# A decoder layer in float32 on one core: an order of issue worked out by the kernel itself, and 130 k pairs by seven products in place of 36

## The chip, the core and the metric

The program runs on one NeuronCore of one Trainium2 chip. A core has a matrix engine (TensorE, PE in the profile), a vector engine (VectorE, DVE), an activation engine (ScalarE, ACT), a general engine (GpSimd, POOL) and an engine that issues transfers (SyncE, SP). Each engine takes its own list of instructions strictly in the order of the program; semaphores hold an instruction back until its inputs are there and its output buffer is free. SBUF is the on-chip memory with 128 partitions, PSUM holds the sums of TensorE in eight banks of 128 x 512 float32 values. The metric is the device time of one execution in microseconds (us), the median over several.

## The reference, cut to what is computed

One layer on 256 tokens with `D = 2048`. All is float32.

```python
h = rmsnorm(x, g_mix)
x_r, g_r, q, k, v, gate_r, gate_a = split(h @ w_in)      # 2816, 2816, then five of 2048
xc = causal_depthwise_conv(x_r, conv_w, conv_b)
y_r = (gelu(g_r) * rg_lru(xc, ...)) @ w_rnn_out          # gates by block-diagonal weights, then a scan over time
q, k = head_rmsnorm(q, q_gain), head_rmsnorm(k, k_gain)  # 16 heads of 128
y_a = stick_breaking_attention(q, k, v) @ w_attn_out
x = x + (sigmoid(gate_r) * y_r + sigmoid(gate_a) * y_a) @ w_o
g, u = split(rmsnorm(x, g_ffn) @ w_ffn_gu)               # 2 x 5632
x = x + (silu(g) * u) @ w_ffn_down
x = x + sigmoid(rmsnorm(x, g_ple) @ w_ple_gate) * (p @ w_ple_proj)
```

Some 350 MB of weights are read once, for 256 tokens.

## The kernel before

**A product of two float32 numbers in three.** TensorE reads float32 operands in a rounded form (`F32R`). Every operand is therefore split into a high part (`AF.Copy` on ScalarE into an `F32R` tile) and a low part (the difference, on VectorE), and a product is the sum of three: high by high, high by low, low by high. For the weights this happens on the chip: `Stream` walks over `CHUNKS` (eight weight tiles of 128 x 128, 512 KB), `dma_to` issues the loads on SP into `p32` (4 buffers), `split_to` issues the two splits into `phl` (4 buffers for each half; lines 230 and 231), `need` keeps the loads 4 and the splits 3 chunks ahead of the use. Weights are packed on the host in the order of `PLAN`.

**Two ways to multiply.** In the recurrent part (x_r and g_r, 22 column tiles each) the weights are stationary: `dense` multiplies a weight tile by 512 columns (the high and low part of 256 tokens, line 425) and its low part by 256 (line 429). The gates (`rnn_gates`) use `mm3` (lines 407 to 409, 256 columns). Everything else has the tokens stationary: `prod` (lines 495 to 497) loads 128 tokens of one k tile as the stationary operand and streams 512 columns of weights, three matmuls for one product. A `group` is 1024 columns of the output: four PSUM banks `q2, q4, q3, q8` (two halves of columns by two halves of tokens), and for each of its k tiles four products.

**Seven products in place of eight.** Two neighbouring k tiles and the two halves of columns make a 2 x 2 block of weights; with the two halves of tokens that is eight products. Strassen's scheme in Winograd's form makes it seven, with sums of weights. `half_sums` forms the sums of tokens; the sums of weights come from transfers that add (`add`, line 214: a load on GpSimd's queue with `accum_op` into the tile that has just been split). In a group that has it, two k pairs are done so (`QP`, by default pairs 2 and 3): slots `"11", "22", "T1", "21", "T2", "T3", "T4"` among the plain slots of `SEVEN`, `SEVEN_FIRST` and `LONG`, each slot one chunk of 1024 columns and two products. Four more PSUM banks (`late`) hold the products that several outputs need, and five VectorE additions and a copy join them at `"T3"`. 18 groups have it: both of `ro`, `v` and `wo`, all 11 of `gu` and the first of `pg`. q, k, the two gates, `ao` and `dn` are plain.

**Order.** The code issues in the order of its loops: the recurrent pairs with four gate blocks among them, `ro`, `v`, q and k blocks with the attention's four steps hooked in by `ATT_AT`, the gate, `ao`, `wo`, the FFN (`gu` and `dn` in four quarters), `pg`. The framework (`schedule_with_timeline_sim=True`) then shifts instructions by its own model. Tiles come from pools by kind (`NT`: A, B, C, X, T), each with its number of buffers. Nine matmuls on zeros (line 537) stand ahead of the first product.

## Time and profile before

| | |
|---|---|
| median of 3 runs | 1896.65 us (1896.46 to 1898.97) |
| the profiled execution's own time | 1897.7 us |
| its span in the trace | 1895.9 us |
| mean granted TensorE clock | 0.999 |
| instructions in the trace | 24167 |
| HBM read, written | 386.00 MB, 2.10 MB |

The page gives each engine's busy time, a strip of 40 slices, the DMA queues, the chain of work that ended last, and the costliest groups of instructions. A group's row names line, engine, operation, `out<-in` by the program's tiles, the shape and the count, then busy time and the mean duration of one, then the engine's idle time just before these instructions and what ended it. Durations overlap: a matmul of 512 columns is shown with 390 ns, while the next one starts 227 ns after it; what an engine can do is read from the distance of starts. TensorE's weight loads (PEld) run beside its matmuls. A few records of matmuls can be missing.

### The profile page before, as it was taken

To read this page: it belongs to the slowest core of one execution; us is meant where nothing else is said; L and a number is where in the kernel's file an instruction comes from. 1 tells how busy PE (TensorE), PEld (TensorE's weight loads), DVE (VectorE), ACT (ScalarE), POOL (GpSimd) and SP (SyncE) were. 2 spreads that over 40 slices of the span, in tenths; PEclk is the share of its full clock that TensorE was granted. 3 is DMA by queue.
4 is the path that set the end of the run, shared out by engine and by line. 5 is a ranking of instruction groups with operands and counts; after the bars stand their busy time and mean duration, and the time that the engine had idled before them with its cause. 6 is when DMAs were issued, how large, how long until landed. Compare 5 with 4: busy or idle time off the path is not lost.

```text
span 1895.9 us, 24167 instructions
## 1 busy us (share of the span) xinstructions
PE 1883.8 (99%) x9045; PEld 1583.6 (84%) x9045; DVE 1274.3 (67%) x1546; ACT 1112.1 (59%) x1447; POOL 63.6 (3%) x81
## 2 busy tenths in 40 slices
PE   8999999999999999999999999999999999999998
PEld 7988888888888888888888888888888888888887
DVE  7867686866766576665567776665666566665674
ACT  7878686874455576676345665543554355544663
POOL 0000000000010000000000000000000000000000
PEclk9999999999999999999999999999999999999999
DMA  7565556677777554555677878776887688766674
GB/s 246 179 199 189 196 176 192 208 234 211 243 202 211 190 166 157 166 156 178 198 269 208 251 227 239 223 222 190 233 236 220 190 232 232 204 196 191 212 201 152
DMA packets 109557, 389.69 MB, mean 206 GB/s; under 512 B 12288, under 2 KB 12672, under 8 KB 109440
## 3 DMA queue, kind: packets, MB, share of 16 engines
q1 hardware_dynamic: 98928, 350.38, 55.4%
q0 software_dynamic: 10368, 37.75, 11.8%
q8 instruction: 71, 1.16, 0.2%
q14 instruction: 46, 0.38, 0.1%
q10 hardware_dynamic: 144, 0.01, 0.0%
HBM read 386.00 MB, written 2.10 MB: 205 GB/s over the span
## 4 chain that ended last, share of the span: by engine, by line
PE 97%; DVE 1%; ACT 1%; DMA 1%; issue 0%; SPq 0%; DVEq 0%; ACTq 0%
PE ps L496 26%; PE ps L495 26%; PE ps L497 26%; PE ps L425 8%; PE ps L429 4%; PE ps L408 1%; PE ps L409 1%; PE ps L407 1%; PE ps L994 1%; DMA w<-in_w_dram 0%; PE ps L934 0%; PE ps L785 0%; DVE T L300 0%; ACT L306 0%; ACT T L306 0%
## 5 line engine op out<-in xcount | busy, mean ns | idle before, releaser
L231 DVE TENSOR_TENSOR wlo<-w,whi 128x1024 fp32r<-128x1024 f32 (+3 forms) x606 | 731.3, 1215 | 426.3 <-ACT whi L230 424.8
L230 ACT ACTIVATE whi<-w 128x1024 fp32r<-128x1024 f32 (+3 forms) x606 | 635.3, 1053 | 560.1 <-PE ps L497 494.5
L496 PE MATMUL ps<-wlo,B 128*128 128x512 f32 x1130 | 440.7, 390 | 0.2 <-DVE wlo L231 0.2
L497 PE MATMUL ps<-whi,B 128*128 128x512 f32 x1130 | 440.4, 390 | 0.0
L495 PE MATMUL ps<-whi,B 128*128 128x512 f32 x1130 | 390.8, 392 | 0.0
L496 PE MATMUL ps<-wlo,A 128*128 128x512 f32 x946 | 368.9, 390 | 0.0
L497 PE MATMUL ps<-whi,A 128*128 128x512 f32 x946 | 368.2, 390 | 0.0
L495 PE MATMUL ps<-whi,A 128*128 128x512 f32 x946 | 352.7, 391 | 0.0
L497 PEld LDWEIGHTS ps<-whi,B 128*128 128x128 f32 x1130 | 212.2, 188 | 44.0
L496 PEld LDWEIGHTS ps<-wlo,B 128*128 128x128 f32 x1130 | 212.3, 188 | 43.6 <-DVE wlo L231 0.7
L495 PEld LDWEIGHTS ps<-whi,B 128*128 128x128 f32 x1130 | 212.2, 188 | 43.7
L497 PEld LDWEIGHTS ps<-whi,A 128*128 128x128 f32 x946 | 177.6, 188 | 36.9
L495 PEld LDWEIGHTS ps<-whi,A 128*128 128x128 f32 x946 | 177.7, 188 | 36.3
L496 PEld LDWEIGHTS ps<-wlo,A 128*128 128x128 f32 x946 | 177.7, 188 | 35.9 <-DVE wlo L231 0.4
L231 DVE TENSOR_TENSOR wlo<-X,whi 128x1024 fp32r<-128x1024 f32 x126 | 154.3, 1224 | 66.8 <-ACT whi L230 62.0
L230 ACT ACTIVATE whi<-X 128x1024 fp32r<-128x1024 f32 x126 | 133.7, 1061 | 93.1 <-PE ps L497 55.7
L425 PE MATMUL ps<-A,whi 128*128 128x512 f32 x704 | 171.0, 392 | 1.7 <-ACT whi L230 1.7
L425 PEld LDWEIGHTS ps<-A,whi 128*128 128x128 f32 x704 | 129.2, 189 | 26.9 <-ACT whi L230 2.1
L214 POOL DMA_DIRECT2D X<-in_w_dram x72 | 61.4, 853 | 1752.2 <-DVE wlo L231 1577.7
L300 DVE TENSOR_TENSOR T<-ps,T 128x512 f32<-128x512 f32 (+1 forms) x160 | 91.1, 610 | 27.6 <-ACT T L306 16.1
L429 PEld LDWEIGHTS ps<-A,wlo 128*128 128x128 f32 x704 | 90.5, 191 | 7.1 <-DVE wlo L231 3.5
L429 PE MATMUL ps<-A,wlo 128*128 128x256 f32 x704 | 92.2, 283 | 2.9 <-DVE wlo L231 2.9
(158 smaller groups left out, 1419.8 us busy)
## 6 DMA issues: line engine op xcount, KB each, us to landing
w<-in_w_dram SPq DMA_DIRECT2D x584, 512.0 KB, 4.1
X<-in_w_dram POOLq DMA_DIRECT2D x72, 512.0 KB, 5.5
X<-in_w_dram SPq DMA_DIRECT2D x54, 512.0 KB, 5.1
w<-in_w_dram SPq DMA_DIRECT2D x16, 448.0 KB, 3.2
C<-in_x_dram SPq DMA_DIRECT2D x8, 256.0 KB, 3.8
out_dram<-T SPq DMA_DIRECT2D x8, 256.0 KB, 2.9
C<-in_xT_dram SPq DMA_DIRECT2D x7, 256.0 KB, 7.9
w<-in_w_dram SPq DMA_DIRECT2D x4, 320.0 KB, 3.5
```

The lines of the kernel that those rows point to most:

```text
L214: self.nc.gpsimd.dma_start(self.raw[o], self.src[a], accum_op=ALU.add)
L230: self.hi_ins = self.nc.scalar.activation(hi[:, :c], t[:, :c], AF.Copy)
L231: self.lo_ins = self.nc.vector.tensor_tensor(lo[:, :c], t[:, :c], hi[:, :c].bitcast(F32), ALU.subtract)
L300: nc.vector.tensor_tensor(o, a, b, op)
L407: nc.tensor.matmul(o, wt[0], xh, start=start, stop=False)
L408: nc.tensor.matmul(o, wt[0], xl, start=False, stop=False)
L409: nc.tensor.matmul(o, wt[1], xh, start=False, stop=stop)
L425: nc.tensor.matmul(pss[e], wt[0], rhs(xs, k), start=(k == 0), stop=(k == n - 1))
L429: nc.tensor.matmul(pss[e][:, :256], wt[1], rhs(xs, k)[:, :256], start=False, stop=False)
L495: nc.tensor.matmul(ps, x[0], wh, start=start, stop=False)
L496: nc.tensor.matmul(ps, x[0], wl, start=False, stop=False)
L497: nc.tensor.matmul(ps, x[1], wh, start=False, stop=stop)
```

## The change

The kernel is written anew around the same arithmetic (1103 lines become 1389). What it does:

**An own order.** `build` records every operation as an `Op` in a `Program`: engine, an assumed duration, the tiles that it reads and writes. `deadlines` gives each a due time from TensorE's order, `schedule` plays the five engines and one transfer server against these durations and hands out buffers, and `emit` issues the operations sorted by the start found there. The framework's own shifting is off (`manual_schedule`). The assumed durations are constants of the file (`PE_NS`, `LOAD_US`, `ADD_US` and the formulas in `vec` and `act`).

**All stages with tokens stationary.** x_r and g_r become groups too: five groups of 512 + 512 columns and a short one of 256 + 256. Their results have tokens on partitions, so x_r is turned by TensorE before the convolution (`conv`) and g_r before the last product (`finish`), 22 turns of four transposes each. The scale of the first norm is read from x in token layout: eight more loads of 256 KB (`xq`), squared with a row sum. `dense`, `evac`, `scaled`, the norm's matmuls (lines 478 and 565) and the nine matmuls on zeros go.

**130 k pairs by seven products**, in 65 blocks of two pairs (18 before): `CFG` lists them. Now also x_r with g_r (one block in the first group, two in the next four), `ro` (2 blocks in each group), gate_r and `v` (2), q and k (1), gate_a (1), `wo` (1), `gu` (2), `dn` (2, 2 and 1 in its three parts), `pg` (2); only `ao` and the short group have none.

**Half of the sums on VectorE.** Per block of two pairs there were four adding transfers; now there are two (T1 and T3) and two additions of 128 x 1024 on VectorE (T2 and T4, in place).

**One chained bank.** The products for several outputs go into one bank `U`, one after another, and ScalarE or VectorE takes the running sum out between them (`ja`, `je`, `jc`, `jd`): five banks for a group in place of eight.

**One pool.** All tiles of 1024 columns share 42 slots (`L`), all of 512 columns 22 (`H`); the scratch for GpSimd's descriptors is cut to 1024 bytes for each partition (`SCRATCH`). FFN: three parts of 16, 16 and 12 k tiles in place of four.

In the built programs TensorE has 9039 matmuls before and 8478 after (of 512 columns 7437 and 7498, of 256 columns 1238 and 532, of 128 columns 344 and 432), VectorE 1546 and 1887 operations, ScalarE 1299 and 1551 activations with 68 and 57 loads of a function table, GpSimd 72 and 130 adding transfers, SP 687 and 648 transfers. The weight splits go from 732 to 873 of each kind.

```diff
+LOAD_US, ADD_US, DMA_LEAD, DMA_TAIL = 1.575 / 512, 2.96 / 512, 1.3, 1.2
+PE_NS = {512: 0.2268, 256: 0.1200, 128: 0.1090}
...
+    def vec(self, n, emit, reads, writes, pointer=False, single=False, name="", **kw):
+        d = 0.062 + 0.001048 * n * (0.5 if single else 1) + (0.06 if pointer else 0)
+        return self.op("DVE", d, 0.125, emit, reads, writes, name=name, **kw)
...
+def schedule(prog, room, window, lag=0.0):
...
+                if e == "PE":
+                    for _, _, o in ready[e]:
+                        if rank[o.n] - head > window:
+                            break
+                        if can(o):
+                            pick = o
+                            break
...
+    return sorted(prog.ops, key=lambda o: (o.start, o.n))
...
-    def add(self, mode):
-
-        m, o, a = {"11": ("T1", "11", "T1"), "T1": ("T2", "11", "22"), "T2": ("T4", "11", "21"),
-                   "22": ("T3", "22", "T1")}.get(mode, (None,) * 3)
-        if m:
-            self.nc.gpsimd.dma_start(self.raw[o], self.src[a], accum_op=ALU.add)
-            self.raw[m] = self.raw[o]
...
+    def group(w, cols, ks, pairs, sums, tokens, how, hooks=None, lead=0):
...
+        q2, q4, q3, q8 = (psum("q") for _ in range(4))
+        U = psum("u") if nd else None
...
+            if m in ("T1", "T3"):
+                if how(m) == "dma":
+                    pr.add(raw.all, chain["b12", dp], 512, name="add")
...
+            if m in ("T2", "T4"):
+                other = chain["22" if m == "T2" else "21", dp]
+                tt(raw.all, raw.all, other.all, ALU.add, name="sum")
+            w_ = weights(raw, 1024, "s")
...
+                    if m == "11":
+                        a = tile("ja", "H")
+                        act(a.all, U.all, AF.Copy, name="ja")
+                    elif m == "T1":
+                        e = tile("je", "H")
+                        tt(e.all, a.all, U.all, ALU.subtract, name="je")
...
-    warm = psum()
-    for i in range(9):
-        nc.tensor.matmul(warm, ones_r, w1t[0], start=True, stop=True)
...
-        for c in range(nc_):
...
-            for f in ((low, wide) if c % 2 or c == nc_ - 1 else (wide, low)):
...
+    for b in range(NBK):
+        xr_group(b, 4, later_hooks(b))
...
-QP = {"ro": (7, 8)}
+CFG = dict(lead=8, x=[4, 5, 6, 7], xr=[[6, 7]] + [[4, 5, 6, 7]] * 4, ro=[0, 1, 2, 3], gtr=[4, 5, 6, 7], v=[4, 5, 6, 7], qk=[4, 5], gta=[4, 5],
+           ao=[], wo=[0, 1], gu=[0, 1, 2, 3], dn=[[0, 1, 2, 3], [8, 9, 10, 11], [16, 17]], pg=[0, 1, 2, 3],
+           how=lambda m: "dma", att0=4, every=9, at=(0, 4, 10, 16), turn=[4, 5, 6, 7])
+SCRATCH = 1024
+ROOM = {"L": 42, "H": 22, "P": 8}
+WINDOW = 60
...
-    with _tile.TileContext(nc, schedule_with_timeline_sim=True) as tc:
-        tile_hybrid_block(tc, *args)
+    with _tile.TileContext(nc) as tc:
+        with tc.manual_schedule():
+            trace(nc, tc, pr, order, args)
```

## The prediction, made blind

> **What bounds the kernel now.** First the page: the engines' busy time, then the chain that ended last.

> ```profile
> span 1895.9 us, 24167 instructions
> PE 1883.8 (99%) x9045; PEld 1583.6 (84%) x9045; DVE 1274.3 (67%) x1546; ACT 1112.1 (59%) x1447; POOL 63.6 (3%) x81
> PE 97%; DVE 1%; ACT 1%; DMA 1%; issue 0%; SPq 0%; DVEq 0%; ACTq 0%
> PE ps L496 26%; PE ps L495 26%; PE ps L497 26%; PE ps L425 8%; PE ps L429 4%; PE ps L408 1%; PE ps L409 1%; PE ps L407 1%; PE ps L994 1%; DMA w<-in_w_dram 0%; PE ps L934 0%; PE ps L785 0%; DVE T L300 0%; ACT L306 0%; ACT T L306 0%
> ```

> TensorE is the bound, and 97% of the chain is its matmuls. A busy TensorE can still be one that runs slowly, so next the groups by shape, for counts, and the chain and the timeline, for the distance of starts.

> ```profile
> L496 PE MATMUL ps<-wlo,B 128*128 128x512 f32 x1130 | 440.7, 390 | 0.2 <-DVE wlo L231 0.2
> L496 PE MATMUL ps<-wlo,A 128*128 128x512 f32 x946 | 368.9, 390 | 0.0
> L425 PE MATMUL ps<-A,whi 128*128 128x512 f32 x704 | 171.0, 392 | 1.7 <-ACT whi L230 1.7
> L429 PE MATMUL ps<-A,wlo 128*128 128x256 f32 x704 | 92.2, 283 | 2.9 <-DVE wlo L231 2.9
> L496 PE MATMUL ps<-wlo,X 128*128 128x512 f32 x160 | 62.4, 390 | 0.8 <-DVE wlo L231 0.8
> ```

> ```profile
> 38.52 3.65 PE ps L425 x16
> 42.17 1.91 PE ps L429 x16
> ...
> 653.97 1.03 PE L785 MATMUL ps<-ident,T 128*128 128x128 f32 x8
> ...
> 1433.24 1.07 PE L495 MATMUL ps<-whi,B 128*128 128x512 f32 x4
> ```

> A 512-column matmul starts (1.07 - 0.39) / 3 = 0.227 us after the one before, a product of three takes 0.68 us. Sixteen stationary weight tiles take 3.65 + 1.91 = 5.56 us. A transpose takes (1.03 - 0.27) / 7 = 0.109 us (0.27 is one alone). Before has 1130 + 946 + 160 = 2236 products: 1520 us of the span at a pace that does not vary. So time changes through the number of matmuls, or where something makes TensorE wait.

> **The change part by part: matmuls.** Seven products for eight: a block of two k pairs and 1024 columns costs 14 products in place of 16. There are 65 blocks, 18 before: 47 x 2 x 0.68 = 63.9 us less. x_r and g_r with tokens stationary: their 704 weight tiles cost 44 x 5.56 = 244.6 us now and 88 chunks of four products, 239.4 us, then: 5.2 less. The turns that this needs: 22 x 4 transposes x 0.109 = 9.6 more. The norm's matmuls go:

> ```profile
> L478 PE MATMUL ps<-acc,ones 128*128 128x256 f32 x4 | 1.0, 379 | 0.0
> L565 PE MATMUL ps<-ones,acc 128*128 128x2 f32 x8 | 0.9, 240 | 0.0
> ```

> 1.9 less. Together -61.4 us. The counts agree: 2494 products then, 7482 matmuls, against 6708 + 704 of that width and 704 narrow ones. Gates and attention are unchanged. From the span that makes 1895.9 - 61.4 = 1834.5 us, if TensorE waits no more than today.

> **Start and end.**

> ```profile
> 1.55 4.18 PE L537 MATMUL ps<-w1h,ones_r 128*128 128x512 f32 x9 [1.55 <-DVE ones_r L347]
> 5.53 1.36 PE L425 MATMUL ps<-A,whi 128*128 128x512 f32 x4
> ...
> 10.89 2.11 PE L425 MATMUL ps<-A,whi 128*128 128x512 f32 x8 [1.67 <-ACT whi L230]
> ...
> 14.80 1.22 PE L429 MATMUL ps<-A,wlo 128*128 128x256 f32 x8 [0.86 <-DVE wlo L231]
> ...
> 28.05 1.21 PE L429 MATMUL ps<-A,wlo 128*128 128x256 f32 x8 [1.86 <-DVE wlo L231]
> ```

> ```profile
> w<-in_w_dram SPq DMA_DIRECT2D x584, 512.0 KB, 4.1
> ```

> Real work starts at 5.53 now. Then the first product needs a whole 512 KB chunk, split high and low: issue at about 0.8, landing 4.1, and about 1.0 and 1.2 for the two splits, so 7.2: 1.7 more. The nine matmuls on zeros ran (4.18 - 0.64) / 8 = 0.44 us apart, half the later pace, and the next four still (1.36 - 0.39) / 3 = 0.32. That slow opening of some 4.5 us falls on products now: 4.5 x (1 - 0.227 / 0.44) = 2.2 us. I take 2.2; 0 is the lower end (the opening passes in time that TensorE waits anyway), twice that the upper (a long early wait brings it back). [...] The end is the same work: last matmul at 1890.6, then two VectorE operations and a store, 5 us.

> **What hides the rest: VectorE.** It gets 141 more weight splits, 130 sums of weights and the joins.

> ```profile
> L231 DVE TENSOR_TENSOR wlo<-w,whi 128x1024 fp32r<-128x1024 f32 x584 | 709.5, 1223 | 413.1 <-ACT whi L230 411.7
> L642 DVE TENSOR_TENSOR_SCAN T<-T,T 128x256 f32<-128x256 f32 x22 | 14.0, 677 | 0.2
> ...
> L230 ACT ACTIVATE whi<-w 128x1024 fp32r<-128x1024 f32 x584 | 616.5, 1060 | 550.1 <-PE ps L497 494.5 <-DVE wlo L231 16.6 <-PE ps L425 16.1
> L306 ACT ACT_TABLE_LOAD x66 | 84.7, 1283 | 2.7 <-DVE cT L533 1.5
> ```

> ```profile
> 1108.64 1.28 DVE L300 TENSOR_TENSOR T<-ps,T 128x512 f32<-128x512 f32 x2
> 1109.84 3.49 DVE L231 TENSOR_TENSOR wlo<-w,whi 128x1024 fp32r<-128x1024 f32 x3
> ```

> Back to back a 1024-column operation takes (3.49 - 1.22) / 2 = 1.135 us, one of 512 columns 1.28 - 0.68 = 0.60; I price others along that line, scans at 0.59. In all that is 1563 us then, 85% of 1840. But by stage, from the order of the changed program: beside TensorE's first 250 us of matmuls stand 126 splits, 18 sums (163 us) and 225 smaller operations (90 us), 253 us of VectorE's. After that it has slack: 41 to 46 us for each 50, then 38, later 83 to 84 of 100. So for 250 us (x_r and g_r with two blocks of seven each, convolution, gates, scan) VectorE has no room. It cannot start on weights before about 5.9 and is through at 5.9 + 253 = 259 plus what it idles; TensorE alone is at 7.2 + 2.2 + 250 = 259. Each microsecond that VectorE idles there is TensorE's.

> ```profile
> 0.00:400.00 400.00, 393.86 (x2250) 347.10 (x2251) 295.74 (x449) 304.62 (x425) 2.16 (x9) 1.00 0.61 200
> ...
> 10.00:50.00 40.00, 36.40 (x207) 31.84 (x208) 35.26 (x57) 29.71 (x49) 0.00 (x0) 1.00 0.66 240
> ...
> 15.00:20.00 5.00, 5.00 (x29) 4.35 (x29) 4.98 (x10) 4.88 (x11) 0.00 (x0) 1.00 1.02 397
> 20.00:25.00 5.00, 5.00 (x30) 4.39 (x29) 4.69 (x8) 5.00 (x10) 0.00 (x0) 1.00 0.64 236
> 25.00:30.00 5.00, 3.14 (x22) 2.76 (x21) 4.79 (x7) 3.81 (x5) 0.00 (x0) 1.00 0.19 55
> ...
> 40.00:45.00 5.00, 5.00 (x31) 4.47 (x30) 5.00 (x11) 3.12 (x4) 0.00 (x0) 1.00 0.52 175
> 45.00:50.00 5.00, 5.00 (x32) 4.44 (x31) 5.00 (x12) 2.75 (x5) 0.00 (x0) 1.00 0.44 151
> ```

> The third number is VectorE's busy time. In the five windows in which it had a queue it idled 0.54 of 25 us, 2.2%; in all of 10 to 50, 12%. On 253 us that is 5.6 and 34. ScalarE, which must deliver the high half first, is not free either: the 126 high halves there at 0.95 back to back (1.06 less 0.11 that overlaps), some 71 us of other activations and 29 function table loads at 1.28 make 228 of the 250. I take 12: nearer the lower end, since a backlog makes an engine run back to back, but not at it, since every high half that comes late idles a VectorE without reserve. Later stalls I cost at nothing: past TensorE's 420 us a split stands, in the issue order, at least 2 us and mostly 8 to 25 us of matmuls ahead of its use; without that lead a late chunk would cost its delay in full.

> **Transfers.**

> ```profile
> q1 hardware_dynamic: 98928, 350.38, 55.4%
> q0 software_dynamic: 10368, 37.75, 11.8%
> ```

> ```profile
> L214 POOL DMA_DIRECT2D X<-in_w_dram x72: 843/851/1003, 406.0 to 1815.5; - x72
> DMA to landing us min/median/max: 5.1/5.5/7.9
> ...
> ACT whi L230 <- DMA X<-in_w_dram: 31.7, 23, 2.8
> ```

> A plain 512 KB costs all 16 engines 0.554 x 1895.9 / 350.38 x 0.524 = 1.57 us, an adding one 0.118 x 1895.9 / 72 = 3.1 us. Then: 330 MB plain, 990 us, and 130 adding, 404 us: 76% of 1840, 67% today. In the first 100 us: 51 units plain, x twice among them, and 8 adding: 105 us, all of the capacity. I cost it at nothing: by the window at 15 us the engines moved 397 GB/s at full share, 1.32 us for a unit, and 92 us for the lot. [...]

> The chained bank: its next product stands behind at least one plain chunk (2.7 us) or another block's, longer than a 0.6 us eviction: nothing. Groups hold five banks, not eight: nothing.

> **Sum.** 1834.5 + 1.7 + 2.2 + 12 = 1850.4 us of span; the median of the runs lies 0.75 above the profiled span: 1851 us. One core's runs spread by 0.1%, so I call 0.2% (3.8 us) the least that shows.

> **Rivals.**

> 1. Transfers pace the first 100 us. Over the first 35 us now, with loads queued, the engines' mean share was 0.75. At that share 105 us take 140, some 31 more than the 109 that TensorE needs, in place of the 12, for VectorE gets its queue by that: 1870. For: share 0.19 at 25 us with TensorE waiting. Against: it was buffers there, not bandwidth.

> 2. Slower: VectorE keeps its idle share in the first 250 us. In the first 400 us now it idles 104 us, 26%, mostly waiting for ScalarE's half of a chunk. With that share 253 us of work take 342: 83 more in place of 12, 1922. It decides from an idle share of 18.5%, where 57 us eat the gain. For: VectorE waits there before almost each split today. Against: it waits because buffers come free late, at TensorE's pace.

> 3. The saving isn't had, because a block of seven is VectorE's: 7 splits and 2 sums, 9 x 1.135 = 10.2 us, against 14 x 0.68 = 9.5 of TensorE. Without carry-over from plain chunks each block loses 0.7: 65 x 0.7 = 45 in place of the 12, and 1884. Against: the lead past 420 us.

> 4. Adding transfers land late. 23 of 72 now make ScalarE wait, 1.4 us each, none TensorE. At that rate 41 of 130, 57 us; were all to reach TensorE: 1908. Against: the same leads.

> **Chances.** Forecast 0.66 (alone 1836 to 1866), rival 1 0.14, rival 2 0.08, rival 3 0.07, rival 4 0.05. Low end 1834: a free opening and hardly a wait for VectorE, less than today's waits of TensorE (4.4 us in the rows above). High end 1884: rival 1, VectorE's 34 with the doubled opening (1875), and rival 3 up to its full price; outside are rivals 2 and 4 and the tails. Faster: 0.66 + 0.14 + 0.06 = 0.86; slower 0.08 + 0.04 = 0.12; same 0.02.

> **What would show it.** Matmuls of 512 columns 0.227 us apart, 7482 in products; VectorE above 95% busy to 250 us and near 85% after; TensorE's waits put down to the splits, within the first 250 us, some 15 to 20 us in all, few after 420. It is wrong if TensorE waits for transfers or adds, if waits spread over the FFN, or if the pace itself changes.

## The result and the profile after

| | before | after |
|---|---|---|
| median of the runs | 1896.8 us (1896.5 to 1899.0, 4 runs) | 1877.0 us (1874.2 to 1878.5, 4 runs) |
| after / before, 95% interval | | 0.9891 [0.9874, 0.9909] |
| span of the profiled execution | 1895.9 us | 1872.4 us |

The kernel is 19.8 us (1.0%) faster, where 45.7 were forecast. The page of the changed kernel, its lines on the span, the engines, the queue of the adding transfers and the two splits of sums:

```profile
span 1872.4 us, 23719 instructions
...
PE 1832.8 (98%) x8478; PEld 1523.6 (81%) x8478; DVE 1602.2 (86%) x1887; ACT 1277.0 (68%) x1696; POOL 115.5 (6%) x139
...
q0 software_dynamic: 18720, 68.17, 20.2%
...
L175 ACT ACTIVATE shi<-r 128x1024 fp32r<-128x1024 f32 x455 | 472.7, 1054 | 250.6 <-DMA r<-in_w_dram 117.6
L142 DVE TENSOR_TENSOR slo<-r,shi 128x1024 fp32r<-128x1024 f32 x455 | 546.7, 1218 | 112.7 <-ACT shi L175 98.9
```

TensorE is 98% busy still, with 567 matmuls fewer; VectorE is at 86% (67% before). ScalarE now stands 117.6 us waiting for adding transfers, and VectorE 98.9 us for ScalarE behind that. Which of it reaches TensorE is in the view of waits (what waited, for what: us in all, times, longest):

```profile
PE rg L799 <- ACT rr L175: 12.0, 9, 3.7
PE q L210 <- ACT xg L175: 6.1, 1, 6.1
PE gut L221 <- DVE jc L146: 5.4, 2, 2.8
PE rg L799 <- ACT ri L175: 2.8, 5, 0.6
PE u L210 <- ACT ja L175: 2.7, 1, 2.7
PE q L211 <- DVE wlo L142: 2.4, 1, 2.4
PE u L211 <- DVE slo L142: 2.0, 3, 1.3
```

The 6.1 is the start. Of the rest only 4.4 us are the late splits of weights that the forecast spoke of; 14.8 us are gate matmuls that wait for a sigmoid, and 8.1 us are three single stalls in the FFN.

Waits do not carry all of it. So here is an account of every microsecond, from the starts of all matmuls: 0.2267 us to the next start for 512 columns, 0.120 for 256, 0.109 for 128 or less are counted as work, and what lies between two starts beyond that as lost.

| us | before | after | difference | forecast |
|---|---|---|---|---|
| matmuls at full pace, without the nine on zeros | 1873.0 | 1812.6 | -60.4 | -61.4 |
| up to 50 us: the time to the first matmul, the nine on zeros (2.0), what is lost | 12.0 | 9.6 | -2.4 | +3.9 |
| lost from 50 to 350 us | 0.9 | 27.6 | +26.7 | +12 |
| lost after 350 us | 4.9 | 17.1 | +12.2 | 0 |
| after the last matmul (its own 0.2267 us counted as work) | 5.1 | 5.5 | +0.4 | 0 |
| span | 1895.9 | 1872.4 | -23.5 | -45.5 |

The saving in matmuls is there. It was given back in two places. Counted from start to start, the 14 waits of gate matmuls make 18.5 of the 27.6 us lost between 50 and 350 us, the period of half pace behind the longest of them 1.5, and three late splits 4.9; the rest is spread in tenths of a microsecond.

**The gates.** The timeline of the changed kernel around one pair of gates, ScalarE's rows and then TensorE's (start, length, engine, line, operation; in brackets the idle time before it and what ended it):

```profile
124.22 1.28 ACT L175 ACT_TABLE_LOAD   x1
125.51 0.47 ACT L175 ACTIVATE rr<-rg,prm 128x256 f32<-128x256 f32 x1
127.06 0.47 ACT L175 ACTIVATE rr<-rg,prm 128x256 f32<-128x256 f32 x1 [1.07 <-PE rg L801]
...
126.04 0.39 PE L799 MATMUL rg<-xcs,whi 128*128 128x256 f32 x1 [0.91 <-ACT rr L175]
129.74 0.39 PE L799 MATMUL rg<-xcs,whi 128*128 128x256 f32 x1 [0.56 <-ACT ri L175]
...
198.82 0.38 PE L799 MATMUL rg<-xcs,whi 128*128 128x256 f32 x1 [3.70 <-ACT rr L175]
```

A bank of `rg` holds the sums of two halves, 256 columns each. The kernel's own plan keeps its dependences by columns, so it issues the sigmoid of the first half (125.51) as soon as that half's products are through. The first matmul of the second half starts at 126.04, behind that sigmoid and the table load ahead of it, though it reads nothing of either: it only writes the other half of the bank that the sigmoid reads. In before all four sigmoids stood behind the products of both halves. Of the 11 pairs, 9 have such a wait, some of them two.

**The FFN.** The timeline of one of the three stalls, POOL, ScalarE, VectorE, then TensorE:

```profile
1350.31 1.79 POOL L188 DMA_DIRECT2D r<-in_w_dram  x2 [17.90 <-PE q L212]
...
1357.21 1.06 ACT L175 ACTIVATE shi<-r 128x1024 fp32r<-128x1024 f32 x1 [6.27 <-DMA r<-in_w_dram]
...
1361.19 1.06 ACT L175 ACTIVATE shi<-r 128x1024 fp32r<-128x1024 f32 x1 [2.44 <-DMA r<-in_w_dram]
...
1358.30 1.23 DVE L142 TENSOR_TENSOR slo<-r,shi 128x1024 fp32r<-128x1024 f32 x1 [4.09 <-ACT shi L175]
...
1369.01 0.33 PE L221 MATMUL gut<-ident,jc 128*128 128x128 f32 x1 [2.66 <-DVE jc L146]
...
1370.44 0.63 PE L211 MATMUL q<-wlo,hg 128*128 128x512 f32 x1
1370.87 0.63 PE L212 MATMUL q<-whi,hg 128*128 128x512 f32 x1
```

Two adding transfers are issued one behind the other at 1350.31. Their splits start at 1357.21 and 1361.19, 6.9 us after the first issue and 10.0 after the second (at 1351.2). The plan counts 6.3 us for one alone (0.85 for the issue, 1.3, 2.96, 1.2). ScalarE and VectorE take their work in a fixed order, so VectorE idles 4.09 us at 1354 with other work behind the late split, and the joins at the end of the group come late: TensorE stands 2.66 us at 1366. After that its matmuls start 0.43 us apart instead of 0.227. The same happens at 1620 and 1708 us; the three places cost some 14.6 us, of which 3 x 1.7 are the low pace behind the stall.

### The profile page after: what moved, and what is told of

It reads as the page before. It is cut to its first block, busy times and chain, and to the rows that moved or that the text cites. A ratio compares the mean times of both kernels' runs of the same rounds, so it can differ in the third digit from the quotient of the medians.

```text
span 1872.4 us, 23719 instructions
## 1 busy us (share of the span) xinstructions
PE 1832.8 (98%) x8478; PEld 1523.6 (81%) x8478; DVE 1602.2 (86%) x1887; ACT 1277.0 (68%) x1696; POOL 115.5 (6%) x139
## 3 DMA queue, kind: packets, MB, share of 16 engines
HBM read 393.86 MB, written 2.10 MB: 211 GB/s over the span
## 5 line engine op out<-in xcount | busy, mean ns | idle before, releaser
L175 ACT ACTIVATE shi<-r 128x1024 fp32r<-128x1024 f32 x455 | 472.7, 1054 | 250.6 <-DMA r<-in_w_dram 117.6
L142 DVE TENSOR_TENSOR slo<-r,shi 128x1024 fp32r<-128x1024 f32 x455 | 546.7, 1218 | 112.7 <-ACT shi L175 98.9
L142 DVE TENSOR_TENSOR wlo<-raw,whi 128x1024 fp32r<-128x1024 f32 (+2 forms) x418 | 499.7, 1206 | 60.8 <-ACT whi L175 49.5
L175 ACT ACTIVATE whi<-raw 128x1024 fp32r<-128x1024 f32 (+2 forms) x418 | 431.5, 1045 | 129.0 <-DMA raw<-in_w_dram 47.6
L210 PE MATMUL q<-whi,xg 128*128 128x512 f32 x624 | 245.4, 393 | 6.1 <-ACT xg L175 6.1
L211 PE MATMUL q<-wlo,xg 128*128 128x512 f32 x624 | 244.2, 391 | 2.5 <-DVE wlo L142 2.4
L212 PE MATMUL q<-whi,xg 128*128 128x512 f32 x624 | 243.9, 391 | 0.0
L142 DVE TENSOR_TENSOR r<-r,r 128x1024 f32<-128x1024 f32 x130 | 157.9, 1219 | 1.2
L210 PEld LDWEIGHTS q<-whi,xg 128*128 128x128 f32 x624 | 117.8, 189 | 29.9 <-ACT xg L175 6.1
L210 PE MATMUL q<-whi,hg 128*128 128x512 f32 x352 | 139.0, 395 | 0.0
L212 PE MATMUL q<-whi,hg 128*128 128x512 f32 x352 | 137.8, 392 | 0.0
L212 PEld LDWEIGHTS q<-whi,xg 128*128 128x128 f32 x624 | 117.7, 189 | 24.7
L210 PEld LDWEIGHTS q<-whi,hg 128*128 128x128 f32 x352 | 66.7, 190 | 13.6
L210 PE MATMUL q<-whi,act 128*128 128x512 f32 x192 | 75.6, 394 | 0.0
L212 PE MATMUL q<-whi,act 128*128 128x512 f32 x192 | 74.8, 390 | 0.0
L175 ACT ACT_TABLE_LOAD x52 | 66.7, 1283 | 2.2 <-PEq L1377 1.2
## 6 DMA issues: line engine op xcount, KB each, us to landing
raw<-in_w_dram SPq DMA_DIRECT2D x396, 512.0 KB, 4.5
r<-in_w_dram SPq DMA_DIRECT2D x195, 512.0 KB, 4.7
r<-in_w_dram POOLq DMA_DIRECT2D x130, 512.0 KB, 7.5
```

Of the source, the lines that this page charges most:

```text
L142: return self.vec(n, lambda nc: nc.vector.tensor_tensor(o.ap(), a.ap(), b.ap(), op), [a, b], [o], name=name, **kw)
L175: nc.scalar.activation(o.ap(), i.ap(), f, **kw)
L210: nc.tensor.matmul(ps.ap(), x[0].ap(), w[0].ap(), start=start, stop=False, **kw)
L211: nc.tensor.matmul(ps.ap(), x[0].ap(), w[1].ap(), start=False, stop=False, **kw)
L212: nc.tensor.matmul(ps.ap(), x[1].ap(), w[0].ap(), start=False, stop=stop, **kw)
```

## Experiments

Times are medians of four to six runs, ratios are to before. Line numbers behind an edit are a few higher than in the changed kernel.

**The sigmoids behind their whole bank.**

```diff
-                act(t[s], pss[w][s], AF.Sigmoid, bias=pc(bias, 2 * p + e), name="sig")
+                act(t[s], pss[w][s], AF.Sigmoid, bias=pc(bias, 2 * p + e), name="sig", also=[pss[w].all])
```

`also` is one more read in the plan's books; the instruction is the same.

> The four sigmoids of the gates are ordered behind the last product into their whole bank, so that no matmul waits for a sigmoid that reads the other half of its bank. Nothing else is edited. Gate theory (most of the 27 us that TensorE loses between 50 and 350 us is that wait): the waits of the gate matmuls for ScalarE, 12.0 and 2.8 us in the changed kernel, go to under 2 us, the half-clock period at 199 us goes, and the time falls by 12 to 18 us, to 1859 to 1865 us. VectorE theory (as predicted: VectorE has no room in the first 250 us): it is the same amount of VectorE work, so TensorE's waits move to the splits, and the time falls by less than 5 us.

1860.1 us (1859.6 to 1866.9), 0.9811 [0.9793, 0.9828]: 16.8 us less than the changed kernel. In its view of waits the one row of a gate matmul is

```profile
PE rg L802 <- DVE wlo L142: 1.7, 1, 1.7
```

No wait of a gate matmul for ScalarE is left, and the period of low pace at 199 us is gone. So the wait was there because of where the sigmoid stood. In the profiles the loss between 50 and 350 us falls from 27.6 to 13.9 us, half of it: splits at 116, 218, 231 and 240 us now come late that did not before. The two profiles are not of like runs, the changed kernel's being its fastest of four and this one the slowest (1866.9 us, the others 1859.6 to 1860.4), with longer stalls in the FFN; so the 16.8 us of the medians carry some uncertainty.

**Four banks in place of two.** The same question from the other side: the sigmoids stay where they are, the halves get banks of their own.

```diff
-                ps = pss[w][e * 256:e * 256 + 256]
+                if (w, e) not in pss:
+                    pss[w, e] = psum("rg")
+                ps = pss[w, e][:256]
```

> Each half of the gates' two sums gets a bank of its own, four banks in place of two; the sigmoids stay ahead of the other half's products, as the changed kernel has them. Theory (a matmul waits because the sigmoid reads the bank that it writes): the waits of gate matmuls for ScalarE go to under 2 us without any sigmoid being moved, and the time falls as with the sigmoids behind the whole bank, to 1857 to 1864 us. Rival (ScalarE is late there whatever the bank, and the table loads with it): the waits stay near 12 us, and the time within 4 us of the changed kernel's 1877.

1864.9 us (1860.8 to 1867.0), 0.9825 [0.9812, 0.9839]. The rows of gate matmuls:

```profile
PE rg L801 <- ACT rr L175: 3.4, 2, 2.4
...
PE rg L802 <- DVE xcs L142: 1.9, 2, 1.0
```

14.8 us of waits for sigmoids became 3.4, and 12.1 us of the time went, without one sigmoid being moved. Both numbers miss the expectation by a little, and why two waits are left was not followed up; but most of the wait hangs on the shared bank. So by the two views of waits the shared bank cost 11.4 of the 14.8 us where the plan reckons by columns.

**Adding transfers 2.5 us longer in the plan**, in their due time and in the time at which the plan sees them land:

```diff
-            o.due -= DMA_LEAD + DMA_TAIL + dma_us(o.size)
+            o.due -= DMA_LEAD + DMA_TAIL + dma_us(o.size) + (2.5 if o.size < 0 else 0)
...
-                    seen = server + DMA_TAIL
+                    seen = server + DMA_TAIL + (2.5 if o.size < 0 else 0)
```

> The plan takes an adding transfer to land 2.5 us later than the changed kernel's plan does (its issue and the splits ahead of it come due 2.5 us earlier). Theory (the three stalls at 1366, 1620 and 1708 us, 14.7 us with their half-clock periods, are adding transfers that land later than planned, behind which ScalarE and VectorE stand in their fixed order): the three stalls go, and the time falls by 10 to 15 us. Rival (the stalls come from VectorE's total load, 86%, wherever the plan puts it): stalls of the same sum turn up at other places, and the time changes by less than 4 us.

1854.0 us (1852.3 to 1855.3), 0.9770 [0.9755, 0.9784]: 23 us less, more than expected. The page has

```profile
L175 ACT ACTIVATE shi<-r 128x1024 fp32r<-128x1024 f32 x455 | 471.9, 1054 | 160.2 <-DMA r<-in_w_dram 49.0
```

ScalarE waits 49.0 us for adding transfers instead of 117.6. The transfers themselves are as long as before (median 7.3 us from issue to landing, 7.5 in the changed kernel). No stall over 1 us is left behind 350 us, and the loss there falls from 17.1 to 5.7 us; between 50 and 350 us, where x_r and g_r add too, it falls from 27.6 to 20.4, and the waits for sigmoids from 14.8 to 10.0. The plan knew how much VectorE had to do; it did not know the transfer.

**The same 1.5 us shorter** (-1.5 in place of 2.5).

> The changed kernel with its plan's adding transfers 1.5 us shorter instead of 2.5 us longer; nothing else. Theory (TensorE stalls late because adding transfers land later than the plan believes): the stalls get more or longer past 1000 us, more than the 14.7 us of the changed kernel, and the time rises by 5 us or more, above 1882 us. Rival (which order the plan happens to give decides, not the length of the transfer): the time moves by less than 4 us or falls.

1887.4 us (1883.5 to 1892.3), 0.9950 [0.9936, 0.9964]: 10.5 us more than the changed kernel. Its view of waits has these rows for TensorE, among others:

```profile
PE gut L221 <- DVE jc L146: 8.6, 2, 4.6
PE u L210 <- ACT ja L175: 5.2, 4, 2.3
PE rg L800 <- DVE xcs L142: 3.6, 1, 3.6
```

The expectation held for the time, and half for the place: behind 1000 us the loss is 18.7 us, 2.9 more than in the changed kernel; the rest came ahead of 350 us and at 494 and 536. The time follows the length that the plan believes, in both directions.

**One block less in groups two to five of x_r and g_r.**

```diff
-xr=[[6, 7]] + [[4, 5, 6, 7]] * 4
+xr=[[6, 7]] + [[4, 5]] * 4
```

> x_r and g_r get one block of seven products each for groups two to five instead of two: 4 blocks fewer, 4 x 2 x 0.68 = 5.4 us more matmuls, and some 6 us less VectorE work for each of the four groups (24 us of the first 250). VectorE theory: the loss between 50 and 350 us, 27 us, falls by 10 us or more, and the time falls by 5 us or more in all. Gate theory: the gate matmuls still wait for the sigmoids, and the time rises by 3 to 6 us.

1874.5 us (1868.4 to 1878.7), 0.9876 [0.9854, 0.9897]: 2.4 us less, and neither theory as stated. The profile tells them apart by place: matmuls at full pace +5.4, the loss up to 350 us from 31.1 to 23.4, the late splits between 47 and 78 us from 5.1 to 1.0. The waits for sigmoids stay at 13.3 us. So VectorE's lack of room is real, and in this pair of profiles it sits ahead of 80 us. Its price is nearer the 4.1 us of the splits than the whole 7.7: the waits for sigmoids are 1.5 us shorter here, and the period of half pace at 199 us, 1.7 us, is not in this profile. The intervals of the two kernels' times overlap, so the 2.4 us alone show nothing.

**Nine matmuls on zeros first.**

```diff
+    wps = tile("warm", "P")
+    pr.mms([(wps.all, ones_r.all, w1t[0].all, 0.0, True, True) for _ in range(9)], [ones_r.all, w1t[0].all], [wps.all],
+           name="warm")
```

> Nine matmuls of 512 columns on zeros are put ahead of the first product, as before had them. They end at about 6 us, where the first product starts. If the half-clock opening costs what the starts of the trace show, the time falls by 2 to 3 us, the first products start 0.227 us apart and the un-throttled clock begins at about 6 us instead of 11.6. Rival: later work in the first 50 us (splits, transfers at 362 GB/s) is the limit there, TensorE gets to the same late split sooner and waits for it, and the time changes by less than 1 us.

1872.9 us (1870.1 to 1875.0), 0.9865 [0.9848, 0.9881]; the interval overlaps that of the changed kernel. In the profile the thirteenth product matmul starts at 9.5 us against 11.7, but at the late splits of 72 and 75 us only 0.5 us of it is left, and the profiled span is 1873.3, 0.9 more than the changed kernel's. The changed kernel's matmuls come in the same order here, so the two can be compared one by one; what follows the late splits is a period of half pace at 77.5 us that the changed kernel's profile does not have. This pair does not decide between the two expectations.

**Whole-bank sigmoids and longer adding transfers together.**

> The gates' sigmoids behind their whole bank and the adding transfers planned 2.5 us longer, together. Theory (two separate losses): the 10.0 us for which gate matmuls still wait for ScalarE in the kernel with the longer adding transfers go, 1854.0 - 10.0 = 1844 us, within 1841 to 1847. Rival (VectorE has no room in the first 250 us, and the gate waits only stand in for its lateness): the waits move to the splits there, and the time stays above 1850 us.

1844.7 us (1843.7 to 1845.6), 0.9719 [0.9706, 0.9732]. All rows of TensorE over 0.2 us:

```profile
PE q L211 <- ACT xg L176: 5.8, 1, 5.8
PE u L212 <- DVE slo L142: 3.5, 4, 1.4
PE q L212 <- DVE wlo L142: 1.8, 3, 0.7
PE rg L802 <- DVE wlo L142: 1.6, 1, 1.6
```

The two losses are separate: 1854.0 less the 10.0 us of sigmoids that were left there. What remains is what the prediction had spoken of, late splits, 6.9 us in all; they come at 60 and 75 us, but also at 117 and 121, at 223 and 227, and at 1269 and 1274. This is 6.4 us under the time forecast for the change.

**And the nine matmuls.**

> As the kernel with both edits, and nine matmuls on zeros ahead of the first product. Theory (the opening's 2 us are given back at the late splits between 55 and 75 us, where VectorE sets the pace): less than 1 us against the kernel with both edits alone. Rival (the opening's loss goes through to the end): 2 us or more.

1844.3 us (1843.6 to 1845.7), 0.9720 [0.9707, 0.9734]: 0.3 us less, as the theory has it. But the profiles do not show its reason. Both kernels issue the same matmuls in the same order: the one with the nine is 2.0 us ahead at 12 us, 1.3 at 60 to 100, behind the late splits, and 1.5 at 221. There a split comes 1.85 us late in place of 1.44, and a period of half pace from 222.70 to 226.11 us, which the other profile does not have, leaves 0.2. Two splits that come late at 1269 and 1274 us only in the other one restore the 2 us to the end (spans 1841.9 and 1843.8 us). So the late splits between 55 and 75 us took some 0.3 us of the gain and small waits ahead of them 0.4, not all of it, and why the medians differ by only 0.3 us stays open.

**And one block less in the second group** (`xr=[[6, 7], [4, 5]] + [[4, 5, 6, 7]] * 3`).

> As the kernel with both edits and the nine matmuls, and one block of seven products less in the second group of x_r and g_r: 1.4 us more matmuls, 6 us less VectorE work ahead of 80 us. Theory (VectorE is without room only up to some 80 us, and the late splits at 55 to 75 us are its whole price): those splits no longer keep TensorE waiting, the opening's 2 us go through too, and the time falls by 3 to 6 us against the kernel with both edits and the nine matmuls, to 1837 to 1841 us. Rival (VectorE has no room for all of the 250 us): the wait turns up behind 100 us, and the time falls by less than 1.5 us.

1837.6 us (1837.0 to 1838.2), 0.9684 [0.9671, 0.9697]: 6.8 us less for 1.4 us more matmuls, a little beyond the 3 to 6 expected. The windows of 50 us, of the changed kernel and then of this one (length; busy time and instructions of PE, PEld, DVE, ACT, POOL; granted clock; share of the DMA engines; GB/s):

```profile
0.00:50.00 50.00, 43.48 (x179) 35.10 (x179) 40.18 (x72) 37.34 (x62) 4.77 (x12) 1.00 0.99 362
50.00:100.00 50.00, 43.88 (x204) 34.86 (x203) 45.98 (x65) 42.24 (x54) 3.28 (x5) 1.00 0.64 188
...
150.00:200.00 50.00, 45.74 (x236) 38.75 (x236) 47.51 (x67) 41.58 (x56) 3.48 (x4) 0.99 0.60 168
```

```profile
50.00:100.00 50.00, 49.72 (x237) 41.51 (x236) 47.81 (x73) 44.96 (x61) 2.60 (x3) 1.00 0.80 240
...
150.00:200.00 50.00, 50.00 (x269) 43.11 (x268) 50.00 (x71) 46.24 (x62) 3.48 (x4) 1.00 0.65 193
```

TensorE loses 0.7 us between 50 and 100 us instead of 8.3. Against the kernel before this last edit the loss falls from 4.3 to 0.7 us there, from 2.6 to 0.2 between 100 and 150, and from 4.0 to 1.4 between 200 and 250, where 1.7 us were the half pace. So the late splits did not end at 80 us, as the theory had it, and room ahead of 80 us took those behind it away as well. And from 150 to 200 us VectorE is busy for the whole window, 50.00 of 50, and TensorE too: VectorE without any reserve costs TensorE nothing there. In the changed kernel it was busy for 47.51 and TensorE for 45.74.

**And ten blocks of seven more behind 400 us**, in q, k, the attention gate, the output projection and the end of the down projection:

```diff
-qk=[4, 5], gta=[4, 5], wo=[0, 1], dn=[[0, 1, 2, 3], [8, 9, 10, 11], [16, 17]]
+qk=[4, 5, 6, 7], gta=[4, 5, 6, 7], wo=[0, 1, 2, 3], dn=[[0, 1, 2, 3], [8, 9, 10, 11], [16, 17, 18, 19]]
```

> As the kernel with four edits (whole-bank sigmoids, adding transfers 2.5 us longer, nine matmuls, one block less in the second group), with ten more blocks of seven products behind 400 us: q and k two in place of one in each of their four groups, the attention gate, the output projection and the last stretch of the FFN's down projection likewise. 10 x 2 x 0.68 = 13.6 us fewer matmuls. Theory (VectorE has room there, and a block costs TensorE nothing but its products): the time falls by 11 to 14 us, to 1824 to 1827 us. Rival (VectorE is without room as soon as attention or the last stretch gets more): waits for splits and scores give back more than half, and the time is above 1830 us.

1829.2 us (1827.5 to 1833.4), 0.9646 [0.9634, 0.9659]: 8.4 us less for 13.6 us fewer matmuls, short of the 11 to 14 expected. The profile has the loss of TensorE at 16.3 us against 12.2, in small waits around 700 to 850, at 1254, 1504 and 1729 us. Its line of engines:

```profile
PE 1813.5 (99%) x8433; PEld 1509.0 (83%) x8433; DVE 1649.6 (90%) x1952; ACT 1300.9 (71%) x1732; POOL 131.0 (7%) x157
```

This is the fastest version, 3.5% under before. With VectorE at 90%, each of the ten blocks brought 0.8 us of its 1.36.

## Why the prediction was off

The direction was right, but only 19.8 of the 45.7 us came. That the time lies in the range owes nothing to the mechanism: the range was made wide by rivals, and the two largest losses are not in the sum. The span missed its forecast by 22.0 us: 14.7 between 50 and 350 us, 12.2 behind, 6.3 the other way in the opening, and 1.4 in the matmuls and the end. By its own steps:

- **Matmuls, -61.4: right** (-60.4). The pace did not change, and the price per block held in two more runs: 24 matmuls more for 4 blocks fewer, and 13.6 us less for ten more.
- **Opening, +3.9: wrong in sign** (-2.4). The first product started at 6.12 us and not at 7.2, and the slow opening up to 11.7 us cost 2.7, near the 2.2 forecast. The upper end of that, a slow opening brought back by a long early wait, showed in neither profile: the granted clock does not change between 11.60 and 199.33 us in the changed kernel, nor between 6.13 and 1893.70 us in before. What was left out is that before, behind its own first product at 5.53, lost another 6.5 us up to 50; 4.4 of them are the waits quoted in the prediction. The changed kernel lost 0.8 there.
- **"Gates and attention are unchanged": this is the step that failed.** The operations are unchanged, their order is not. Putting the first half's sigmoid ahead of the second half's products adds 14 waits, in 9 of the 11 pairs; the prediction listed what moves between engines and looked at the chained bank and at the number of banks, but not at a bank that one engine reads while another is to write it. It cost 14.8 us of waits, 18.5 counted from start to start, and 1.5 to 1.7 of low pace; undone by itself it brought 16.8.
- **VectorE in the first 250 us, +12: cause real, some 4 to 5 us, and in a smaller place.** VectorE was 80 to 95% busy there, not above 95, since it too stood behind ScalarE. In the changed kernel its late splits keep TensorE waiting only up to 80 us, 4.4 us; with the gate waits and the stalls gone they come up to 227 us as well (6.9 us of waits in the kernel with both edits, 1.5 of them behind 1200 us). By the same sign the condition "each microsecond that VectorE idles there is TensorE's" fell: with the other losses gone VectorE was busy 50.00 of 50 us and TensorE lost 0.2.
- **Later stalls, 0: failed,** 12.2 us. The leads of 8 to 25 us are those of the order of issue. They shrink when an adding transfer lands later than the plan believes, because everything behind its split on ScalarE and VectorE waits with it. That is the mechanism of rival 4: 56 waits and 117.6 us on ScalarE where that rival reckoned 41 and 57. Three of them got through, and each was followed by half clock (from 1370.11, 1622.69 and 1711.44 us on, 3.41 us each). Waits in the FFN were among the prediction's own signs of being wrong.
- **Transfers, 0: right.** 0.99 of the engines' time and 362 GB/s over the first 50 us, and between the start and 47 us no wait of TensorE for it; rival 1 fell. Rival 2 fell with VectorE's idle share, 9% over the first 250 us where 18.5 was its mark, and rival 3 with the last experiment: VectorE was busy 90% and the time lower still.
- **The median, +0.75 on the span:** +4.6. The profiled execution was the fastest of four. The changed kernel's runs spread over 4.4 us, those of the kernel 1.5 us further off the transfers' length over 8.8, those with one block less in four groups over 10.3, those of the kernel with four edits over 1.2. The last section gives a reason that fits a part of this and that no run tried by itself.

## What to carry to other kernels

Where a kernel works out its own order, every resource must be in its books in the grain in which its waits come: here PSUM by bank (14.8 us of waits for sigmoids, 3.4 with a bank for each half), and an adding transfer by its measured landing (7.5 us from issue in the median), not by its share of bandwidth. A wrong length can cost far more than its error, because engines that work in a fixed order hold everything behind the late item: 130 transfers planned 2.5 us longer brought 23 us. When a change moves work to an engine that is nearly full, ask first which waits stop that engine; here a full VectorE that was not kept waiting cost nothing for 50 us.

## What the runs showed of the hardware

```profile
73.04:76.45 3.41, 1.66 (x6) 1.05 (x6) 3.41 (x8) 3.41 (x6) 0.00 (x0) 1.00 0.78 225
...
195.92:199.33 3.41, 0.51 (x4) 0.52 (x5) 3.41 (x7) 2.81 (x5) 0.00 (x0) 1.00 0.60 197
199.33:202.75 3.42, 3.42 (x18) 3.42 (x18) 2.10 (x3) 1.42 (x2) 0.00 (x0) 0.50 0.47 153
...
1366.70:1370.11 3.41, 0.76 (x5) 0.57 (x6) 3.41 (x6) 3.35 (x5) 0.00 (x0) 1.00 0.96 169
1370.11:1373.52 3.41, 3.41 (x11) 2.64 (x10) 3.41 (x4) 2.50 (x4) 0.00 (x0) 0.50 0.72 292
1373.52:1376.94 3.42, 3.42 (x19) 2.81 (x18) 3.42 (x4) 1.91 (x3) 0.00 (x0) 1.00 0.28 89
```

Here the windows in which TensorE was busy for 0.51 and 0.76 us were each followed by one at half clock, and behind those, in which it was busy for 3.42 and 3.41 us, the full clock was back. (The first window shown, busy for 1.66 us, was not followed by half clock.) The nearest cases on the two sides, first from the kernel with sigmoids, transfers and the nine matmuls, where half clock followed, then from the one with one block less in four groups, where it did not:

```profile
219.29:222.70 3.41, 1.55 (x7) 0.96 (x7) 3.41 (x9) 3.29 (x7) 0.00 (x0) 1.00 0.00 0
```

```profile
248.27:251.68 3.41, 1.58 (x14) 1.38 (x12) 2.04 (x2) 3.37 (x5) 0.00 (x0) 1.00 0.48 154
```

On its own trace's grid the second begins at 248.29 and is busy for 1.56 us, so the two are all but equal. In the twelve profiles of this case one window at full clock lies on the wrong side of this: in the kernel with whole-bank sigmoids alone, the window from 1858.36 us, in which the last matmul ends, was busy for 1.48 us, and the next one was at full clock:

```profile
1858.36:1861.78 3.42, 1.48 (x7) 0.90 (x5) 2.94 (x5) 0.00 (x0) 0.00 (x0) 1.00 0.55 207
1861.78:1865.19 3.41, 0.00 (x0) 0.00 (x0) 0.00 (x0) 0.00 (x0) 0.00 (x0) 1.00 0.20 77
```

So in these traces the edge lay near 1.5 us (half clock behind 1.55, none behind 1.56 nor, at the end of one span, behind 1.48) and is not known closer. A gap shorter than 3.413 us was enough: one of 2.66 us at 1366 was followed by half clock, and one of about 2.4 us at 75 us in one of the four kernels that have it, the one with nine matmuls on zeros alone. There TensorE was busy for 1.02 us of the window from 74.11 us; in the changed kernel the gap lay across two windows, busy for 1.66 and 2.10 us. The grid's place against the first instruction differed from profile to profile (a change at 6.13 us in before and at 11.60 in the changed kernel, 1.60 steps apart). By an estimate from these numbers a kernel with gaps of 2 to 3 us would draw lots for 1.7 us each, half of 3.413, which fits a part of the spread above. The four runs with one block less in four groups took 1868.4, 1873.5, 1875.6 and 1878.7 us at mean granted clocks of 0.999, 0.995, 0.994 and 0.994; the changed kernel's runs are not in such an order (0.996, 0.994, 0.995, 0.994 from the fastest on). The stalls themselves vary too: the changed kernel and the one with nine matmuls on zeros issue the same products in the same order, and the three in the FFN last 2.66, 2.78 and 2.69 us in one profile, 4.21, 1.90 and 2.49 in the other. A window 45% busy (1.55 of 3.41 us) stood ahead of half clock in two profiles: from 219.29 us in the kernel with sigmoids, transfers and the nine matmuls, as shown, and from 141.66 us in the one with the adding transfers 1.5 us shorter.

**Adding transfers.** With 130 of them in place of 72 the median from issue to landing was 7.5 us against 5.5; a plain transfer of the same 512 KB took 4.5 to 4.7 against 4.1. In the timeline above, the splits behind two that were issued 0.9 us apart started 4.0 us apart.
